# Two buffers for the token sums, and the low part of a pair's sums made inside the next pair's

## The chip, the cores and the metric

The kernel runs on one core of one Trainium2 chip. The metric is the device time of one launch in microseconds (us). Five engines work side by side: TensorE (PE in the views, its weight loads PEld), VectorE (DVE), ScalarE (ACT), GpSimd (POOL) and SyncE (SP), which issues most of the transfers.

## The reference

A decoder trunk over 256 tokens of width 2048: a recurrent block and an attention block, each followed by a dense layer with a squared ReLU (an MLP), all in float32. The change lies in the two MLPs alone:

```
def _mlp(h, w1, w2):
    u = jnp.einsum('bsd,df->bsf', h, w1)        # 2048 -> 8192
    u = jnp.square(jax.nn.relu(u))
    return jnp.einsum('bsf,fd->bsd', u, w2)     # 8192 -> 2048

for i in range(DEPTH):                          # DEPTH = 2
    ...                                         # recurrent block, then attention
    x = x + _mlp(_rmsnorm(x, mlp_norm[i]), mlp_w1[i], mlp_w2[i])
return _rmsnorm(x, final_norm)
```

## The kernel before

**High and low parts.** A float32 product is made of three products of rounded numbers: every operand is cut into a high part (ScalarE copies it into a rounded type, `whi` for a weight) and a low part (VectorE subtracts the high part from the original, `wlo`). `three` and `stand_w` then issue, for each 128 rows of the contraction, high by high, high by low and low by high. A weight comes in *units* of 128 x 2048 (1 MB) in tiles `raw`, or `q...` where sums of weights are made. `before_unit` and `behind_unit` run ahead of the unit in use: transfers five units ahead, `whi` three ahead, `wlo` two ahead. There are three buffers of `whi`, so the `whi` of the unit three places on is written when TensorE has finished the present one.

**The MLP.** It is done in eight parts, p = 0 to 7, of 1024 of the 8192 inner columns. In a *first* (the code's `"w"`, `plan_first`) one unit of w1 gives 128 inner columns for the 256 tokens: 48 matmuls of 256 columns into a bank `g` or `acc`. `u_done` then scales it and takes the ReLU on VectorE (`uu`, L517), squares it on ScalarE and copies the high part (`aT`); `u_low` makes the low part of it on VectorE one item later (L526).

**Sums of tokens and weights.** In parts 0 to 6 the second product is done by a scheme that needs seven products of half blocks where eight would be plain: `plan_group` names them b11, b21, t1, t2, b22, t3, t4, two groups per part, 12 matmuls of 512 columns each. t1, t2, b22 and t3 need sums of quarters of the tokens (s0 to s3), and some need sums of weights (`qT`, `q12`, `q21`, `q22`; L599 on VectorE, L595 by transfers that add). `sums_of_tokens` makes s0 to s3 for one of four pairs k of inner columns: four VectorE instructions of 128 x 128 into `sw`, then `hilo`: ScalarE's copy into the high half of `sT` (L203), and VectorE's subtraction into its low half (L204). `hilo` issues both in one go, so VectorE stands in front of its subtraction until ScalarE has copied. There are 2 MLPs x 7 parts x 4 pairs = 56 such pairs.

**The order** of a part is written out by hand in `ORDER[2]`: first, b11, t1, first, b21, b22, t2, first, t3, first, t4 (that is group 0), then group 1: b11, t1, first, b22, t2, b21, t3, first, first, first, t4. The firsts in it belong to the next part. In the main loop each item issues what runs ahead (`before_unit`), its matmuls (`fn`), `behind_unit`, what earlier items deferred (`after(n, ...)`), and then the sums of every pair that waits. The sums of part p+1 are held back until t3 of group 1 of part p has been issued (`busy`); the sums of pairs 0 and 1 then come together behind t3, those of pair 2 behind the second of the three firsts, and those of pair 3 behind t4, which is three items ahead of the t1 of the next part, where they are first read.

```
    0: ("s", "w") * 8,
    2: (
        "w", "b11 0", "t1 0", "w", "b21 0", "b22 0", "t2 0", "w", "t3 0", "w", "t4 0", "b11 1", "t1 1", "w",
        "b22 1", "t2 1", "b21 1", "t3 1", "w", "w", "w", "t4 1",
    ),
```

Each engine takes its instructions in the order in which they were issued.

Of the kernel before, what the change touches and what calls it, by code (L numbers as in the profile page):

```python
# [10 lines left out]
F32 = mybir.dt.float32  # L11
F32R = mybir.dt.float32r
AF = mybir.ActivationFunctionType
# [55 lines left out]
def trunk(ctx: ExitStack, tc: tile.TileContext, a: dict, out: bass.AP):  # L69
    nc = tc.nc  # L70
    P = 128
# [74 lines left out]
    def before_unit(i):  # L146
        step("load", i + 1 + LOOK_LOAD, load)
        step("make", i + LOOK_HI, make)
        step("hi", i + LOOK_HI, cut_hi)
        step("lo", i + 1 + LOOK_LO, cut_lo)  # L150

    def behind_unit(i):
        step("make", i + 1 + LOOK_HI, make)
        step("hi", i + 1 + LOOK_HI, cut_hi)
# [26 lines left out]
    lru = Scope()  # L181
# [18 lines left out]
    state = {}  # L200

    def hilo(hi_out, lo_out, src):
        nc.scalar.activation(hi_out, src, AF.Copy)  # L203
        nc.vector.tensor_sub(lo_out, src, hi_out.bitcast(F32))  # L204

    def new_xT(n):
        t = perm.tile([P, 4, 512], F32R, name=f"xT{n}")
        state["xT", n] = t
        return t
# [318 lines left out]
    def sums_of_tokens():  # L528

        if not waiting or (busy[0] is not None and busy[0] < waiting[0][0]):  # L530
            return
        p, k = waiting.pop(0)
        uu = squares.pop((p, k))
        (a11, a21), (a12, a22) = ((uu[:, h, 0:128], uu[:, h, 128:256]) for h in range(2))
        w = lru.tile([P, 4, 128], F32, name="sw")
        nc.vector.tensor_sub(w[:, 0], a22, a21)  # L536
        nc.vector.scalar_tensor_tensor(w[:, 1], w[:, 0], -1.0, a11, op0=OP.mult, op1=OP.subtract)  # L537
        nc.vector.scalar_tensor_tensor(w[:, 2], w[:, 1], -1.0, a12, op0=OP.mult, op1=OP.subtract)  # L538
        nc.vector.tensor_sub(w[:, 3], a11, a21)  # L539
        t = lru.tile([P, 8, 128], F32R, name=f"sT{k}")  # L540
        hilo(t[:, 0:4], t[:, 4:8], w)
        state["sT", p, k] = t
        return True

    def standing(p, what):

        def get(k):
            if what[0] == "a":
                t, h = int(what[1]) - 1, int(what[2]) - 1
                x = aT(8 * (p % 2) + 4 * h + k)  # L550
                return x[:, t * 128:(t + 1) * 128], x[:, 256 + t * 128:256 + (t + 1) * 128]
            x = state["sT", p, k]
            return x[:, int(what[1])], x[:, 4 + int(what[1])]
        return get
# [305 lines left out]
    for n in range(NCH):  # L860
        xg[n] = new_xg(n)
        rs = [wts.tile([P, UW], F32, name="raw", bufs=RAW_BUFS) for _ in range(3)] if n == 0 else rs
        for h in range(2 if n == 0 else 1):
            w = 2 if n == 0 else 4
# [10 lines left out]
        t = new_xT(n)  # L875
        for h in range(2 if n == 0 else 1):
            w = 2 if n == 0 else 4
# [76 lines left out]
    for at, (u, fn, kind) in enumerate(items):  # L954
        if u is None:
            fn()
            continue
        before_unit(u)
        state["border"] = kind is None and at + 1 < len(items) and items[at + 1][2] == "w"
        fn()  # L960
        behind_unit(least[at] - 1)
        for f, args in later.pop(now[0], []):
            f(*args)
        while sums_of_tokens():
            pass
        now[0] += 1
# [73 lines left out]
```

## Time and profile before

| | us |
|---|---|
| median of 3 runs (lowest, highest) | 2125.91 (2124.99, 2126.18) |
| the profiled execution | 2125.21 |
| its span, first to last instruction | 2123.4 |
| TensorE busy, of the span | 2096.7 (99%) |
| VectorE busy | 1708.7 (80%) |
| ScalarE busy | 1253.2 (59%) |

The first MLP lies at about 392 to 1059 us of the span, the second runs from about 1453 us to the end. In them a part from 1 on takes 83.04 to 83.3 us. Shares of busy time are means over the span; what holds TensorE up in one place is read from the order of time there.

### The profile page before, as it was taken

What the parts mean: (1) busy time and instruction counts of PE and PEld (TensorE: products, weight loads), DVE (VectorE), ACT (ScalarE), POOL (GpSimd) and SP (SyncE); (2) the same over time, 40 slices, a digit from 0 to 9 for tenths busy, and PEclk for the clock granted to TensorE, in tenths of its full rate; (3) what the DMA queues carried; (4) which work ended last, traced back from release to release, by engine and by line L of the source; (5) the groups of instructions that cost most, each with busy time, mean ns of one, the idle gap of its engine ahead of it and who ended that gap; (6) DMA issues with size and microseconds to landing.
All of it is one profiled execution on the core that took longest, in us unless ns stands there. A gap on an engine that the chain in (4) does not pass through costs nothing.

```text
span 2123.4 us, 32378 instructions
## 1 busy us (share of the span) xinstructions
PE 2096.7 (99%) x13529; PEld 1885.6 (89%) x13529; DVE 1708.7 (80%) x1836; ACT 1253.2 (59%) x1303; POOL 122.2 (6%) x92
## 2 busy tenths in 40 slices
PE   7999999999999999999999999999999999999997
PEld 7999988998989899899888888889989898998996
DVE  8898955699999999998555555556999999999985
ACT  5877755556665656656545544555565656566563
POOL 2121100000000000000000000000000000000002
PEclk9999999999999999999999999999999999999999
DMA  6665555677788778777554454446777887787773
GB/s 227 220 211 192 194 210 183 229 245 239 248 265 264 231 257 265 232 243 239 198 182 163 171 178 163 167 168 245 242 242 246 267 263 230 257 267 231 240 244 139
DMA packets 69778, 472.30 MB, mean 222 GB/s; under 512 B 7680, under 2 KB 8064, under 8 KB 14336
## 3 DMA queue, kind: packets, MB, share of 16 engines
q1 hardware_dynamic: 61568, 411.51, 52.5%
q0 software_dynamic: 8064, 58.72, 14.0%
q8 instruction: 106, 1.74, 0.3%
q14 instruction: 40, 0.33, 0.0%
HBM read 409.39 MB, written 2.10 MB: 194 GB/s over the span
## 4 chain that ended last, share of the span: by engine, by line
PE 64%; DVE 25%; issue 7%; ACT 3%; DMA 0%; SPq 0%; DVEq 0%; ACTq 0%
PE acc L187 42%; PE g L187 13%; DVE wlo L128 13%; PE tr L187 6%; DVE qT L599 3%; DVE xc L603 3%; ACT sT L203 2%; ACT whi L124 1%; DVE uu L517 1%; DVE aT L526 1%; DVE sw L537 1%; DVE sw L538 1%; DVE sw L536 1%; DVE sw L539 0%; DVE sT L204 0%
## 5 line engine op out<-in xcount | busy, mean ns | idle before, releaser
L124 ACT ACTIVATE whi<-raw 128x2048 fp32r<-128x2048 f32 (+2 forms) x306 | 567.1, 1855 | 425.0 <-PE acc L187 304.3
L128 DVE TENSOR_TENSOR wlo<-raw,whi 128x2048 fp32r<-128x2048 f32 (+2 forms) x306 | 683.5, 2238 | 137.1 <-ACT whi L124 136.9
L187 PE MATMUL g<-xT,whi 128*128 128x256 f32 (+1 forms) x3617 | 622.8, 277 | 0.0
L187 PEld LDWEIGHTS g<-xT,whi 128*128 128x128 f32 x3617 | 545.8, 188 | 0.0
L187 PE MATMUL g<-xT,wlo 128*128 128x256 f32 x1808 | 501.4, 277 | 0.8 <-DVE wlo L128 0.8
L187 PEld LDWEIGHTS g<-xT,wlo 128*128 128x128 f32 x1808 | 339.8, 188 | 2.6 <-DVE wlo L128 1.2
L187 PE MATMUL acc<-whi,aT 128*128 128x512 f32 x1056 | 335.0, 391 | 0.0
L187 PE MATMUL acc<-xT,whi 128*128 128x256 f32 x1764 | 303.7, 277 | 3.1 <-DVE xT L881 2.1
L128 DVE TENSOR_TENSOR wlo<-q,whi 128x2048 fp32r<-128x2048 f32 x112 | 256.1, 2287 | 22.5 <-ACT whi L124 22.5
L124 ACT ACTIVATE whi<-q 128x2048 fp32r<-128x2048 f32 x112 | 212.8, 1910 | 103.9 <-PE g L187 91.6
L187 PEld LDWEIGHTS acc<-xT,whi 128*128 128x128 f32 x1764 | 266.9, 188 | 4.8 <-DVE xT L881 2.5
L187 PE MATMUL acc<-xT,wlo 128*128 128x256 f32 x880 | 244.4, 278 | 8.0 <-DVE wlo L128 7.9
L187 PE MATMUL acc<-whi,xT 128*128 128x512 f32 x768 | 245.9, 396 | 0.0
L187 PEld LDWEIGHTS acc<-whi,aT 128*128 128x128 f32 x1056 | 198.3, 188 | 40.8
L187 PE MATMUL acc<-wlo,aT 128*128 128x512 f32 x528 | 205.8, 390 | 0.0
L124 ACT ACTIVATE whi<-qT 128x2048 fp32r<-128x2048 f32 x56 | 107.4, 1918 | 131.3 <-DVE qT L599 71.1
L187 PEld LDWEIGHTS acc<-xT,wlo 128*128 128x128 f32 x880 | 165.9, 189 | 9.3 <-DVE wlo L128 9.3
L187 PEld LDWEIGHTS acc<-whi,xT 128*128 128x128 f32 x768 | 144.3, 188 | 30.7
L187 PE MATMUL acc<-wlo,xT 128*128 128x512 f32 x384 | 150.4, 392 | 0.0
L187 PE MATMUL tr<-whi,sT 128*128 128x512 f32 (+1 forms) x490 | 148.7, 373 | 0.2
L187 PE MATMUL acc<-whi,sT 128*128 128x512 f32 (+1 forms) x476 | 147.9, 378 | 0.0
L187 PE MATMUL tr<-whi,aT 128*128 128x512 f32 (+1 forms) x460 | 145.1, 384 | 0.0
(176 smaller groups left out, 2439.2 us busy)
## 6 DMA issues: line engine op xcount, KB each, us to landing
raw<-in_w SPq DMA_DIRECT2D x172, 1024.0 KB, 5.9
q<-in_w SPq DMA_DIRECT2D x84, 1024.0 KB, 7.0
raw<-in_w_qkv SPq DMA_DIRECT2D x48, 1024.0 KB, 4.8
raw<-in_w_in SPq DMA_DIRECT2D x35, 1024.0 KB, 4.8
q<-q POOLq DMA_DIRECT2D x28, 1024.0 KB, 12.2
q<-qT POOLq DMA_DIRECT2D x28, 1024.0 KB, 7.0
raw<-in_w_out SPq DMA_DIRECT2D x20, 1024.0 KB, 4.7
raw<-in_w_o SPq DMA_DIRECT2D x16, 1024.0 KB, 4.8
```

Source lines behind the costliest of these rows:

```text
L124: nc.scalar.activation(split[i][0][:, s], r, AF.Copy)
L128: nc.vector.tensor_sub(split[i][1][:, s], r, split[i][0][:, s].bitcast(F32))
L187: nc.tensor.matmul(o, l, r, start=start, stop=stop, skip_group_check=True)
L203: nc.scalar.activation(hi_out, src, AF.Copy)
L517: nc.vector.scalar_tensor_tensor(uu, ps[:, :S], 0.0, state["rstdB"], op0=OP.max, op1=OP.mult)
L526: nc.vector.tensor_sub(t[:, 256:512], uu, t[:, 0:256].bitcast(F32))
L536: nc.vector.tensor_sub(w[:, 0], a22, a21)
L537: nc.vector.scalar_tensor_tensor(w[:, 1], w[:, 0], -1.0, a11, op0=OP.mult, op1=OP.subtract)
L538: nc.vector.scalar_tensor_tensor(w[:, 2], w[:, 1], -1.0, a12, op0=OP.mult, op1=OP.subtract)
L599: nc.vector.tensor_add(q[to], q[a], q[b])
L603: (nc.vector.tensor_add if sign > 0 else nc.vector.tensor_sub)(x, x, bank[b])
```

## The change

The tile of the sums gets two buffers. The fourth sum is issued second. ScalarE's copy is issued where it was, but VectorE's subtraction is kept for later: it is issued inside the sums of the next pair, between its third and its last instruction, or, where no sums come before, at the end of the next item.

```
-        w = lru.tile([P, 4, 128], F32, name="sw")
+        w = lru.tile([P, 4, 128], F32, name="sw", bufs=2)
         nc.vector.tensor_sub(w[:, 0], a22, a21)
+        nc.vector.tensor_sub(w[:, 3], a11, a21)
         nc.vector.scalar_tensor_tensor(w[:, 1], w[:, 0], -1.0, a11, op0=OP.mult, op1=OP.subtract)
+        low_of_sums()
         nc.vector.scalar_tensor_tensor(w[:, 2], w[:, 1], -1.0, a12, op0=OP.mult, op1=OP.subtract)
-        nc.vector.tensor_sub(w[:, 3], a11, a21)
         t = lru.tile([P, 8, 128], F32R, name=f"sT{k}")
-        hilo(t[:, 0:4], t[:, 4:8], w)
+        nc.scalar.activation(t[:, 0:4], w, AF.Copy)
         state["sT", p, k] = t
+        state["low"] = (t, w)
         return True
+
+    def low_of_sums():
+        if "low" in state:
+            t, w = state.pop("low")
+            nc.vector.tensor_sub(t[:, 4:8], w, t[:, 0:4].bitcast(F32))
@@ the main loop, behind an item's deferred work
+        low_of_sums()
         while sums_of_tokens():
             pass
```

The order of instructions changes on VectorE alone (elsewhere only line numbers do). At two places it reads as follows; the lines L536 to L550 of the changed kernel are those of the diff, in it L538 and L540 are the two sums that read another sum, L550 is the subtraction that was L204, and L606 and L610 are the former L599 and L603.

VectorE behind t3 of group 1, where pairs 0 (`sT_5095`) and 1 (`sT_5103`) are summed, before:

```order
L536 TENSOR_TENSOR sw<-uu 128x128
L537 SCALAR_TENSOR_TENSOR sw<-sw,uu 128x128
L538 SCALAR_TENSOR_TENSOR sw<-sw,uu 128x128
L539 TENSOR_TENSOR sw<-uu 128x128
L204 TENSOR_TENSOR sT_5095<-sw,sT_5095 128x512
L536 TENSOR_TENSOR sw<-uu 128x128
L537 SCALAR_TENSOR_TENSOR sw<-sw,uu 128x128
L538 SCALAR_TENSOR_TENSOR sw<-sw,uu 128x128
L539 TENSOR_TENSOR sw<-uu 128x128
L204 TENSOR_TENSOR sT_5103<-sw,sT_5103 128x512
L128 TENSOR_TENSOR wlo<-raw,whi 128x2048
L517 SCALAR_TENSOR_TENSOR uu<-g,rstdB 128x256
```

The same place now:

```order
L536 TENSOR_TENSOR sw<-uu 128x128
L537 TENSOR_TENSOR sw<-uu 128x128
L538 SCALAR_TENSOR_TENSOR sw<-sw,uu 128x128
L540 SCALAR_TENSOR_TENSOR sw<-sw,uu 128x128
L536 TENSOR_TENSOR sw<-uu 128x128
L537 TENSOR_TENSOR sw<-uu 128x128
L538 SCALAR_TENSOR_TENSOR sw<-sw,uu 128x128
L550 TENSOR_TENSOR sT_5095<-sw,sT_5095 128x512
L540 SCALAR_TENSOR_TENSOR sw<-sw,uu 128x128
L128 TENSOR_TENSOR wlo<-raw,whi 128x2048
L517 SCALAR_TENSOR_TENSOR uu<-g,rstdB 128x256
L550 TENSOR_TENSOR sT_5103<-sw,sT_5103 128x512
```

Pair 0's subtraction has gone into pair 1's sums, and pair 1's behind the low part of a unit and the ReLU of a first.

VectorE behind t4, where pair 3 (`sT_5322`) is summed, before; `wlo<-qT` is the low part of the unit of the coming t1, `uu` the ReLU of the first ahead of b11 and t1, and `wlo<-raw` the low part of the unit of the first behind t1:

```order
L536 TENSOR_TENSOR sw<-uu 128x128
L537 SCALAR_TENSOR_TENSOR sw<-sw,uu 128x128
L538 SCALAR_TENSOR_TENSOR sw<-sw,uu 128x128
L539 TENSOR_TENSOR sw<-uu 128x128
L204 TENSOR_TENSOR sT_5322<-sw,sT_5322 128x512
L128 TENSOR_TENSOR wlo<-qT,whi 128x2048
L517 SCALAR_TENSOR_TENSOR uu<-g,rstdB 128x256
L128 TENSOR_TENSOR wlo<-raw,whi 128x2048
```

The same place now:

```order
L536 TENSOR_TENSOR sw<-uu 128x128
L537 TENSOR_TENSOR sw<-uu 128x128
L538 SCALAR_TENSOR_TENSOR sw<-sw,uu 128x128
L540 SCALAR_TENSOR_TENSOR sw<-sw,uu 128x128
L128 TENSOR_TENSOR wlo<-qT,whi 128x2048
L517 SCALAR_TENSOR_TENSOR uu<-g,rstdB 128x256
L550 TENSOR_TENSOR sT_5322<-sw,sT_5322 128x512
L128 TENSOR_TENSOR wlo<-raw,whi 128x2048
```

Pair 3's subtraction now stands behind the low part for t1 and behind the ReLU of a first, and still ahead of the low part of the next unit.

## Rows read from the trace of the kernel before

**Rows 1.** The page, busy us, share of the span, instructions.

```profile
PE 2096.7 (99%) x13529; PEld 1885.6 (89%) x13529; DVE 1708.7 (80%) x1836; ACT 1253.2 (59%) x1303; POOL 122.2 (6%) x92
```

**Rows 2.** Windows, one part: its length, then busy us and instructions of each engine.

```profile
533.00:616.10 83.10, 82.88 (x561) 75.28 (x559) 78.13 (x77) 50.26 (x42) 3.42 (x4) 1.00 0.79 253
```

**Rows 3.** Timeline, TensorE, part 1 of the first MLP: start, us, instruction, idle before.

```profile
590.62 0.40 PE L187 MATMUL g<-xT,whi 128*128 128x256 f32 x2
...
596.08 0.39 PE L187 MATMUL tr<-whi,aT 128*128 128x512 f32 x1
...
598.82 0.39 PE L187 MATMUL acc<-whi,sT 128*128 128x512 f32 x1
599.35 0.50 PE L187 MATMUL acc<-wlo,sT 128*128 128x512 f32 x1
599.69 0.62 PE L187 MATMUL acc<-whi,sT 128*128 128x512 f32 x2
600.15 0.40 PE L187 MATMUL acc<-wlo,sT 128*128 128x512 f32 x1
...
610.18 0.39 PE L187 MATMUL acc<-whi,sT 128*128 128x512 f32 x1
610.62 0.50 PE L187 MATMUL acc<-wlo,sT 128*128 128x512 f32 x1
610.96 0.63 PE L187 MATMUL acc<-whi,sT 128*128 128x512 f32 x2
...
615.98 0.40 PE L187 MATMUL g<-xT,whi 128*128 128x256 f32 x2
616.29 0.38 PE L187 MATMUL g<-xT,wlo 128*128 128x256 f32 x1
616.51 0.40 PE L187 MATMUL g<-xT,whi 128*128 128x256 f32 x2
```

**Rows 4.** Timeline, TensorE, the first behind the first t1 of an MLP.

```profile
435.48 0.40 PE L187 MATMUL g<-xT,whi 128*128 128x256 f32 x2
436.27 0.39 PE L187 MATMUL g<-xT,wlo 128*128 128x256 f32 x1 [0.39 <-DVE wlo L128]
436.49 0.40 PE L187 MATMUL g<-xT,whi 128*128 128x256 f32 x2
```

**Rows 5.** Waits of TensorE's weight loads, 392 to 1004 us: total us, times, longest.

```profile
PEld acc L187 <- DVE wlo L128: 6.2, 12, 0.6
...
PEld g L187 <- DVE wlo L128: 0.6, 1, 0.6
```

**Rows 6.** Timeline, VectorE, the places of rows 3 and 4.

```profile
433.32 0.69 DVE L204 TENSOR_TENSOR sT<-sw,sT 128x512 fp32r<-128x512 f32 x1 [1.63 <-ACT sT L203]
...
595.42 0.28 DVE L539 TENSOR_TENSOR sw<-uu 128x128 f32<-128x128 f32 x1
596.40 0.69 DVE L204 TENSOR_TENSOR sT<-sw,sT 128x512 fp32r<-128x512 f32 x1 [0.70 <-ACT sT L203]
597.01 2.29 DVE L128 TENSOR_TENSOR wlo<-qT,whi 128x2048 fp32r<-128x2048 f32 x1
599.21 0.42 DVE L517 SCALAR_TENSOR_TENSOR uu<-g,rstdB 128x256 f32<-128x256 f32 x1
599.55 2.28 DVE L128 TENSOR_TENSOR wlo<-raw,whi 128x2048 fp32r<-128x2048 f32 x1
...
608.28 2.29 DVE L128 TENSOR_TENSOR wlo<-q,whi 128x2048 fp32r<-128x2048 f32 x1
...
613.95 2.29 DVE L128 TENSOR_TENSOR wlo<-raw,whi 128x2048 fp32r<-128x2048 f32 x1
```

**Rows 7.** The tile of the sums: ScalarE's copy (ns least/median/most), and who waited for it.

```profile
L203 ACT ACTIVATE sT<-sw x56: 615/632/636, 400.0 to 1990.5; 128x512 fp32r<-128x512 f32 x56
...
  DVE sT L204: 43.9, 56
```

**Rows 8.** Timeline, ScalarE, behind the copy of pair 3: the unit of the first behind t1.

```profile
596.27 1.91 ACT L124 ACTIVATE whi<-raw 128x2048 fp32r<-128x2048 f32 x1
```

## The prediction

> **What bounds the kernel now.** I read the page first: matmuls fill 99% of the span [rows 1], so the time is TensorE's, and only what makes its matmuls start earlier can change it. The windows by part come second. In one part of an MLP the matmuls are busy 82.88 of 83.10 us [rows 2]: 0.22 us of idle, which looks like no room. But a matmul's row is longer than its turn. At an even pace two matmuls of 512 columns start 0.46 us apart (599.69 to 600.15), 0.23 each, though a row lasts 0.39; and the 48 matmuls of a first take 596.08 - 590.62 = 5.46 us, 0.114 each, though one lasts 0.28 [rows 3]. A stall of a few tenths hides under the row in front of it. So the third view is the starts in the timeline, and there one part stalls at three places [rows 3]:
>
> - at t1 of group 0, 598.82 to 599.69 is 0.87 us for two matmuls that should take 0.46: 0.41 lost;
> - at b22 of group 0, 610.18 to 610.96 is 0.78 for 0.46: 0.32 lost;
> - at the first behind t2, 615.98 to 616.51 is 0.53 for three of 0.114: 0.19 lost.
>
> Each time the matmul that starts late reads `wlo`, and VectorE has just finished that tile: 597.01 + 2.29 = 599.30 against a start at 599.35; 608.28 + 2.29 = 610.57 against 610.62; 613.95 + 2.29 = 616.24 against 616.29 [rows 3, 6]. In each of the three the matmul after the late one is about 0.11 late as well; I count that in. In part 0 of an MLP there is one larger stall instead, in the first behind t1: 435.48 to 436.49 is 1.01 us for three matmuls, 0.67 lost [rows 4].
>
> The waits of the weight loads say how often: in the first MLP 12 on `wlo` for a bank `acc` and one for `g` [rows 5], that is two in each of parts 1 to 6 and the one of part 0; the second MLP has the same counts. (That view does not list the third, which is short.)
>
> Why is VectorE late? In front of each pair's subtraction it stands still for ScalarE's copy: 43.9 us in 56 pairs [rows 7], mostly 0.70, at the start of an MLP up to 1.63 [rows 6]. Around t1 it is the engine that is behind: the first ended on TensorE at 596.08 [rows 3], and VectorE comes to its ReLU at 599.21 [rows 6], 3.1 us later, with no idle row between 596.40 and there.
>
> **The change, part by part.**
>
> *The second buffer of `sw`* issues nothing. It lets pair 1's sums be written while pair 0's still wait to be subtracted. It costs room only.
>
> *The fourth sum moved to second place.* The same four instructions stand ahead of ScalarE's copy. The bounds are nothing and its whole 0.28 us [rows 6] per pair. I take nothing: what counts below does not need it.
>
> *The subtraction moved.* 56 x 0.69 us of work remain, none is added. Pair 0's now follows three of pair 1's sums, at some 0.28 each, which is 0.6 to 0.9 us behind the start of a copy that takes 0.63 [rows 6, 7]: a rest of 0 to 0.1 us in place of 0.70. Those of pairs 1 to 3 come a `wlo` (2.29) later, when the copy is long done: nothing left. So up to 2.8 us per part of standing still goes, over the four pairs.
>
> *At t1.* The least that must happen: of the four pairs only the last counts, VectorE being no earlier up to 595.70 (595.42 + 0.28). Then `wlo<-qT` starts there and not at 597.01, since both the 0.70 and the subtraction (596.40 to 597.01, 0.61 of queue) stood ahead of it [rows 6]. It ends at 597.99. TensorE wants it at 598.82 + 0.23 = 599.05 [rows 3]: 1.06 us to spare, the 0.41 goes. At the most it starts 2.8 + 0.61 = 3.4 us earlier.
>
> *Behind it* stand the ReLU and the subtraction of pair 3, then `wlo<-raw` for the first behind t1, at 599.55 now. By the least case the ReLU starts at 597.90 (0.09 before the end of `wlo<-qT`, as 599.21 to 599.30 now), the subtraction at 598.24, `wlo<-raw` at 598.85: 0.70 earlier [rows 6]. At the most it is bounded by ScalarE: the `whi` of this unit can start when TensorE has finished the first, 596.08, a little before its 596.27 now, and takes 1.91 [rows 3, 8], so it starts at about 598.05: 1.5 earlier. From there on I take VectorE's work as unchanged down to 613.95, so 0.7 to 1.5 us is what b22 and the next first may use. TensorE comes to b22 0.41 earlier and VectorE was 610.62 - 610.41 = 0.21 late there: 0.62 is needed, and either case gives it. At the first behind t2 TensorE comes 0.73 earlier, and VectorE was about 0.08 late (616.29 against 615.98 + 2 x 0.114): 0.81 is needed, which the least case misses by 0.1 and the most meets by 0.7. The pairs before the last have 2.1 us of waits to give, and their being of no use at all is unlikely; I take the most.
>
> *In part 0* VectorE waits 1.63 us in front of pair 3's subtraction [rows 6], and that subtraction too goes behind the ReLU, so `wlo<-raw` may come up to 1.63 + 0.61 = 2.2 us earlier. TensorE's stall there is 436.27 - 435.71 = 0.56 plus 0.11 [rows 4]: it goes.
>
> *The moved subtraction itself* is now late by how much? Pair 3 is read by the fourth quarter of t1, its low half by the last matmul of that: 598.82 + 11 x 0.23 = 601.3. By the least case it is done at 598.24 + 0.69 = 598.93. It is queued behind the ReLU, which waits for the first on TensorE (596.08): no matter, that is 1.8 us earlier than 597.90. It costs nothing while those 2.4 us last.
>
> **A rule and the rows.** The rows of busy time give an idle of 0.22 us a part, the starts give 0.41 + 0.32 + 0.19 = 0.92. The Trainium skill, Perfetto Trace Analysis (Identifying the Most-Contended Engine), says that busy time of matmuls is a poor measure of how near TensorE is to its limit, as they are pipelined. By that, this trace agrees: rows of 0.39 us start 0.23 apart. The busy rows would make the sum 14 x 0.22 = 3 us, the starts make it the one below.
>
> **The sum.** 12 parts (1 to 6 of both MLPs) x 0.92 = 11.0 us, taking the part of rows 3 for all, and 2 x 0.67 = 1.3 for part 0: 12.3 us off 2125.21, the profiled execution, whose span is 2123.4 (1.8 us lie outside it). The median of the runs is 0.7 higher, 2125.91; on that scale 2113.6.
>
> **The rivals.**
>
> *VectorE's freed time comes back as other waits (B).* Once it is no longer behind, it must wait for TensorE's results and ScalarE's `whi`, and b22 and the next first are left as they were; t1 and part 0 alone gain. For it: the earliest start of `wlo<-raw` is set by ScalarE. Against it: even the least case met b22. 12 x 0.41 + 1.3 = 6.2 us: 2119.7.
>
> *The change does not do what it says (C): nothing moves.* The waits of VectorE have cover after all, or the stalls pass to another late tile at the same places. For it: the idle of TensorE in the windows is 0.22 us a part, and 14 x 0.22 = 3.1 us is then all that there is, 2122.8 at best, which is within 0.2% (4.3 us, about what a measurement of this kernel can tell from no change). Against it: three ends of `wlo` that lie 0.05 us before three late starts. The Trainium skill, VectorE: DVE Perf Modes (Rules for kernel authors), advises to reduce the number of operations and not of semaphores; by that this change, which removes no operation, gives 0 and 2125.9. The trace does not agree where the semaphore is another engine's: 43.9 us of VectorE's idle stand in front of these 56 operations [rows 7].
>
> *Slower (D): the low half of pair 3 comes too late for t1.* It now stands behind a ReLU that needs TensorE's last first. VectorE is 3.1 us behind TensorE there at present; if, in the new order, it were over 2.4 us later than in my least case, t1 would stop in its fourth quarter in each of 12 parts. One us past that point is 12 us: 2137.9. Against it: nothing in the order lengthens VectorE's queue ahead of that place.
>
> **Chances.** The forecast 0.64, B 0.19, C 0.11, D 0.06. The predicted time is that of the forecast, 2113.6; its own range, by a third stall that stays in part (12 x 0.1) and by stalls up to 0.1 larger or smaller in the other parts, is 2111.5 to 2116. The range for 8 in 10 reaches up to B: 2111.5 to 2120. Faster by over 0.2% are the forecast and B, 0.83; within 0.2% C, 0.11; slower D, 0.06.
>
> **What will show it.** In the changed kernel's timeline: no idle of some 0.7 us ahead of L550; `wlo<-qT` ending over 1 us before t1's second matmul; the two matmuls at t1 and at b22 0.46 us apart and not 0.87 and 0.78; the waits of weight loads on `wlo` gone from both MLPs; a part of 82.1 to 82.4 us where it had 83.04 to 83.3. If t1 is clean and b22 is not, B holds. If VectorE's idle moves in front of `uu` or `wlo` and the starts of TensorE stay as they are, C. If t1's last matmul waits for L550, D. The prediction would be wrong above all if another engine, ScalarE's `whi` or a transfer, is close behind VectorE at these places, where no row of before shows by how much.

## The result, and the profile after

The changed kernel takes 2114.3 us (median of 4 runs, 2113.44 to 2115.05) beside 2125.97 of the kernel before: a ratio of 0.9945, 95% interval 0.9929 to 0.9961, 11.7 us less. 2113.6 was forecast. The chips of the experiments further down gave the kernel before 2123.4 to 2124.1, so runs are compared by their ratio to it on the same chip.

The page after, and the window of one part of the first MLP (from the three firsts in a row to the next three; columns as in [rows 2]):

```profile
PE 2090.8 (99%) x13529; PEld 1890.9 (89%) x13529; DVE 1703.0 (81%) x1836; ACT 1255.8 (59%) x1303; POOL 122.2 (6%) x92
```

```profile
490.78:572.89 82.11, 82.09 (x560) 75.38 (x559) 77.67 (x77) 50.47 (x42) 3.41 (x4) 1.00 0.80 256
```

A part that took 83.10 us [rows 2] takes 82.11, and TensorE's idle time in it is all but gone. VectorE still issues 77 instructions in a part; its busy time falls by 0.46 us (78.13 to 77.67), about what the shorter sums of four pairs save (4 x 0.12, worked out further down). VectorE's waits in one part, first before (488.44 to 571.54 us), then after (490.78 to 572.89): total us, times, longest:

```profile
DVE sT L204 <- ACT sT L203: 2.8, 4, 0.7
DVE wlo L128 <- ACT whi L124: 1.9, 3, 1.4
```

```profile
DVE wlo L128 <- ACT whi L124: 3.2, 5, 1.4
DVE uu L517 <- PE g L187: 1.1, 3, 0.4
```

So VectorE stands still almost as long as before, 4.3 us in place of 4.7, but at other places, where in parts 1 to 6 no matmul comes to wait for it. The timeline of TensorE at the three places of [rows 3], in the same part:

```profile
600.16 0.39 PE L187 MATMUL acc<-whi,sT 128*128 128x512 f32 x1
600.39 0.39 PE L187 MATMUL acc<-wlo,sT 128*128 128x512 f32 x1
600.62 0.62 PE L187 MATMUL acc<-whi,sT 128*128 128x512 f32 x2
...
611.08 0.39 PE L187 MATMUL acc<-whi,sT 128*128 128x512 f32 x1
611.31 0.39 PE L187 MATMUL acc<-wlo,sT 128*128 128x512 f32 x1
611.54 0.62 PE L187 MATMUL acc<-whi,sT 128*128 128x512 f32 x2
...
616.53 0.40 PE L187 MATMUL g<-xT,whi 128*128 128x256 f32 x2
616.77 0.28 PE L187 MATMUL g<-xT,wlo 128*128 128x256 f32 x1
616.89 0.39 PE L187 MATMUL g<-xT,whi 128*128 128x256 f32 x2
```

The starts at t1 and b22 are 0.46 us apart where they were 0.87 and 0.78, at the next first 0.36 where they were 0.53. VectorE there, which answers to [rows 6]:

```profile
575.44 0.29 DVE L536 TENSOR_TENSOR sw<-uu 128x128 f32<-128x128 f32 x1
575.64 0.29 DVE L537 TENSOR_TENSOR sw<-uu 128x128 f32<-128x128 f32 x1
575.84 0.30 DVE L538 SCALAR_TENSOR_TENSOR sw<-sw,uu 128x128 f32<-128x128 f32 x1
576.17 0.29 DVE L540 SCALAR_TENSOR_TENSOR sw<-sw,uu 128x128 f32<-128x128 f32 x1
...
594.98 2.28 DVE L128 TENSOR_TENSOR wlo<-qT,whi 128x2048 fp32r<-128x2048 f32 x1
597.63 0.42 DVE L517 SCALAR_TENSOR_TENSOR uu<-g,rstdB 128x256 f32<-128x256 f32 x1 [0.36 <-PE g L187]
597.97 0.68 DVE L550 TENSOR_TENSOR sT<-sw,sT 128x512 fp32r<-128x512 f32 x1
599.47 2.29 DVE L128 TENSOR_TENSOR wlo<-raw,whi 128x2048 fp32r<-128x2048 f32 x1 [0.81 <-ACT whi L124]
...
608.21 2.29 DVE L128 TENSOR_TENSOR wlo<-q,whi 128x2048 fp32r<-128x2048 f32 x1
...
613.87 2.29 DVE L128 TENSOR_TENSOR wlo<-raw,whi 128x2048 fp32r<-128x2048 f32 x1
```

The ReLU (L517) now waits 0.36 us for TensorE, where VectorE came to it 3.1 us late: it has caught up. No subtraction (L550) has more than 0.1 us of idle ahead of it. The low parts end ahead of their matmuls: 594.98 + 2.28 = 597.26 against 600.39, 610.50 against 611.31, 616.16 against 616.77.

The waits of the weight loads, 392 to 1004 us, which answer to [rows 5]:

```profile
PEld tr L187 <- issue: 2.9, 7, 0.4
PEld acc L187 <- DVE sT L550: 0.9, 1, 0.9
```

No wait on `wlo` is left, but there is a new one, once in each MLP: t1 of part 0 waits for the moved subtraction. TensorE and VectorE there:

```profile
437.18 0.39 PE L187 MATMUL acc<-wlo,sT 128*128 128x512 f32 x1
438.10 0.50 PE L187 MATMUL acc<-whi,sT 128*128 128x256 f32 x2 [0.53 <-DVE sT L550]
```

```profile
436.76 0.68 DVE L610 TENSOR_TENSOR xc<-xc,tr 128x512 f32<-128x512 f32 x1
437.36 0.69 DVE L550 TENSOR_TENSOR sT<-sw,sT 128x512 fp32r<-128x512 f32 x1
```

From 437.18 to 438.10 is 0.92 us for one matmul of 0.23, and the one behind is late by 0.11: 0.80 lost, where part 0 had lost 0.67 in the first behind t1 [rows 4].

### The profile page after: what moved, and what is told of

Read it like the earlier page. It is cut to its first block, busy times and chain, and to the rows that moved or that the text cites. A ratio compares the mean times of both kernels' runs of the same rounds, so it can differ in the third digit from the quotient of the medians.

```text
span 2113.0 us, 32396 instructions
## 1 busy us (share of the span) xinstructions
PE 2090.8 (99%) x13529; PEld 1890.9 (89%) x13529; DVE 1703.0 (81%) x1836; ACT 1255.8 (59%) x1303; POOL 122.2 (6%) x92
## 4 chain that ended last, share of the span: by engine, by line
PE 96%; DVE 2%; ACT 1%; issue 0%; DMA 0%; SPq 0%; DVEq 0%; ACTq 0%
PE acc L187 49%; PE g L187 30%; PE tr L187 14%; DVE wlo L128 1%; PE tr L228 0%; ACT whi L124 0%; DVE xT L888 0%; PE tr L704 0%; PE g L712 0%; DMA raw<-in_w_in 0%; PE tr L735 0%; PE g L745 0%; PE g L711 0%; PE g L744 0%; PE g L743 0%
## 5 line engine op out<-in xcount | busy, mean ns | idle before, releaser
L187 PE MATMUL acc<-xT,whi 128*128 128x256 f32 x1764 | 308.2, 280 | 2.3 <-ACT whi L124 1.5
```

The source lines that it names most:

```text
L187: nc.tensor.matmul(o, l, r, start=start, stop=stop, skip_group_check=True)
```

## The experiments

All are edits of the changed kernel. The length of a part is taken, as above, between the starts of the three firsts in a row; there are six such lengths in each MLP, and they hold parts 1 to 6. "Lost" compares with 82.12.

| run | median us | before beside it | ratio (95%) | a part, us |
|---|---|---|---|---|
| before | | | 1 | 83.10 to 83.30 |
| changed | 2114.3 | 2125.97 | 0.9945 (0.9929 to 0.9961) | 82.11 to 82.13 |
| changed, again | 2111.39 | 2123.43 | 0.9940 (0.9927 to 0.9954) | 82.10 to 82.14 |
| no delay | 2116.41 | 2124.11 | 0.9963 (0.9951 to 0.9976) | 82.47 to 82.51 |
| last pair | 2111.36 | 2124.11 | 0.9938 (0.9926 to 0.9951) | 82.11 to 82.13 |
| first pairs | 2110.87 | 2124.11 | 0.9943 (0.9930 to 0.9955) | 82.11 to 82.13 |
| old order | 2113.23 | 2123.43 | 0.9946 (0.9933 to 0.9958) | 82.09 to 82.13 |
| one buffer | 2114.21 | 2124.08 | 0.9951 (0.9938 to 0.9964) | 82.09 to 82.13 |
| one more | 2111.81 | 2124.08 | 0.9941 (0.9927 to 0.9955) | 82.09 to 82.13 |
| two more | 2150.12 | 2124.08 | 1.0120 (1.0105 to 1.0134) | 84.94 to 85.19 |
| item later | 2128.83 | 2124.08 | 1.0023 (1.0014 to 1.0033) | 83.47 to 83.77 |
| ahead | 2110.32 | 2124.11 | 0.9933 (0.9920 to 0.9947) | 82.13 |
| ahead, again | 2109.45 | 2123.43 | 0.9930 (0.9918 to 0.9942) | 82.10 to 82.14 |
| take later | 2106.77 | 2123.43 | 0.9918 (0.9904 to 0.9931) | 81.84 to 81.87 |

**No delay.** The two buffers and the new order alone.

```
-        nc.scalar.activation(t[:, 0:4], w, AF.Copy)
+        hilo(t[:, 0:4], t[:, 4:8], w)
-        state["low"] = (t, w)
```

> The two buffers and the new order of the four sums stay, but each pair's subtraction is issued right behind ScalarE's copy again. My theory: from the sums of tokens to the first behind t2 VectorE's queue is the late one, and what counts is how much earlier it gets. The four waits of 0.70 us come back; the new order alone makes the sums of a pair shorter (start of the first to the end of the last: 1.14 us before, 1.02 in the changed kernel), 0.48 a part. That covers t1 (0.31 late) and leaves b22 0.14 late instead of 0.21: some 0.4 us a part lost where it was 0.92, so about 2120, with idle of 0.7 us ahead of each subtraction and a clean t1. Rival: the order of the sums is worth nothing and the delay is all: 2125.9, t1 stalls 0.4 us.

VectorE, then TensorE at t1, then the waits of weight loads from 392 to 1004 us:

```profile
596.59 0.69 DVE L204 TENSOR_TENSOR sT<-sw,sT 128x512 fp32r<-128x512 f32 x1 [0.70 <-ACT sT L203]
597.20 2.28 DVE L128 TENSOR_TENSOR wlo<-qT,whi 128x2048 fp32r<-128x2048 f32 x1
```

```profile
599.64 0.39 PE L187 MATMUL acc<-whi,sT 128*128 128x512 f32 x1
599.87 0.39 PE L187 MATMUL acc<-wlo,sT 128*128 128x512 f32 x1
```

```profile
PEld acc L187 <- DVE wlo L128: 1.7, 6, 0.3
```

The 0.70 is back and t1 is clean all the same: 597.20 + 2.28 = 599.48 against 599.87. Of the 12 waits on `wlo` for a bank `acc` the six short ones at b22 are left; b22 loses 0.15 to 0.21 us there and the first behind t2 0.16 to 0.20. A part loses 0.35 to 0.39 us, as my theory had it (0.4). The order of four small instructions is worth 0.6 to 0.8 us a part, three fifths and more of the whole.

**Last pair, first pairs.** The subtraction is delayed for one kind of pair only; for the others it is issued at once.

```
         state["low"] = (t, w)
+        if k < 3:              # first pairs: k == 3
+            low_of_sums()
```

> The subtraction is kept for later for the last pair of four alone; pairs 0 to 2 are subtracted at once. My theory: with the new order of the sums (0.48 us a part) and the last pair's 0.70 and 0.61 out of the way, VectorE is 1.2 to 1.8 us earlier, and t1, b22 and the next first need at most 0.81: parts 1 to 6 are as clean as in the changed kernel, 2114.3, although three of four waits are back. Rival: each wait is worth its quarter of the gain: 2114.3 + 3/4 of 11.7 = 2123.

> The reverse: pairs 0 to 2 are subtracted later, the last pair at once. My theory: VectorE has caught up by the last pair's sums, so wlo for t1 ends 1.31 us later than in the changed kernel, about 1.8 us ahead of its matmul in place of 3.1, and the wlo behind it waits for ScalarE anyway: parts 1 to 6 stay clean. In part 0 the subtraction in the middle of t1 no longer waits (0.80 us lost there in the changed kernel, twice), but the first behind t1 stalls by about 0.55 again: 2113.5 to 2114.3. Rival: the wait of the last pair is the one that counts, as the least case of the prediction had it: t1 and b22 stall again, 2122 or more.

Both have parts of 82.11 to 82.13 us: three of the four waits may come back, or the last alone, and nothing shows. With the new order there is room for either. So the rivals of both, that each wait has its quarter of the gain or that the last one has it all, have fallen for a kernel that has the new order; with the old order the two were not tried. In part 0 the two differ as expected: the first stalls in t1 by 0.80 us, as the changed kernel does, the second in the first behind t1 by 0.67.

**Old order.** The delay with the four sums as they were.

```
-        nc.vector.tensor_sub(w[:, 3], a11, a21)
         ...
         nc.vector.scalar_tensor_tensor(w[:, 2], w[:, 1], -1.0, a12, op0=OP.mult, op1=OP.subtract)
+        nc.vector.tensor_sub(w[:, 3], a11, a21)
```

> The changed kernel with the four sums in their old order (the fourth last), the rest of the change kept. My theory: the delayed subtraction alone makes VectorE 1.3 us and more earlier at t1 and behind it, which is enough for all three places: parts 1 to 6 of 82.1 us as in the changed kernel, no measurable difference to it. Rival: the gain is that of the new order, which alone gave two thirds of it: about 2121 on a chip where the kernel before takes 2126.

0.9946, parts as clean: the delay is enough without the order. Each half of the change buys most of what the other does, and the two gains don't add up.

**One buffer.** The subtraction goes ahead of the next pair's sums, so the two pairs that come together wait once.

```
+        low_of_sums()
-        w = lru.tile([P, 4, 128], F32, name="sw", bufs=2)
+        w = lru.tile([P, 4, 128], F32, name="sw")
         ...
-        low_of_sums()
```

> One buffer of the sums again; a pair's subtraction is issued right ahead of the next pair's sums and not inside them. My theory: only the two pairs that come together lose something, 0.70 us of VectorE's queue in each part, which the slack behind it holds: 2114.3. Rival: the second buffer and the place in the middle are what the change is worth: 2118 or more.

The parts are those of the changed kernel: neither the second buffer nor the place in the middle of the sums is needed for the gain.

**One more, two more.** Idle work on VectorE behind each pair's sums, into a tile that nobody reads then.

```
+        spare = perm.tile([P, 512], mybir.dt.bfloat16, name="junk")
+        for _ in range(1):     # two more: 2
+            nc.vector.tensor_sub(spare.rearrange("p (q c) -> p q c", q=4), w, w)
```

> The changed kernel, with one more VectorE operation of 128 x 512 (0.69 us, 0.61 of queue) behind each pair's sums, whose result nobody reads. My theory: 2.4 us of queue a part come back, as much as the waits were, but VectorE has 1.9 us of idle in that stretch now (0.26, 0.49, 0.36 and 0.81): it is about 0.5 us later where b22 has 0.8 and the next first 0.6 us of slack. Parts 1 to 6 stay clean or nearly so; part 0 loses 0.6 more, twice: 2114.5 to 2117. Rival: VectorE's busy time sets the pace, and 56 x 0.61 us come on top: 2148. Another: queue taken by work undoes the change as the waits did: 2125.

> The same with two such operations behind each pair's sums, 4.9 us of queue a part. My theory: now the slack is gone: wlo for t1 comes about 1.0 us late, that for b22 1.0 more, the next first 0.2, with 0.1 us behind each: some 2.5 us in each of 12 parts and 2.4 us in part 0 together: about 2147. Rival: VectorE's idle elsewhere in the part takes it up, 2117 or less.

56 operations of 0.69 us cost the parts nothing; 112 cost 2.8 to 3.1 us a part. VectorE and TensorE at t1 with two more:

```profile
602.91 2.28 DVE L128 TENSOR_TENSOR wlo<-qT,whi 128x2048 fp32r<-128x2048 f32 x1
```

```profile
603.40 0.39 PE L187 MATMUL acc<-whi,sT 128*128 128x512 f32 x1
605.25 0.50 PE L187 MATMUL acc<-wlo,sT 128*128 128x512 f32 x1 [1.46 <-DVE wlo L128]
```

The low part ends at 605.19 and the matmul that wants it starts at 605.25, 1.6 us late (1.0 was expected). So it is VectorE's queue that sets the stalls, waits and work alike, and the change has bought a slack of at least one such operation per pair and less than two.

**Item later.** In parts 1 to 6 the left-over subtraction waits one item more.

```
+        state["due"] = now[0] + (2 if p else 1)
-        low_of_sums()
+        if now[0] >= state.get("due", 0):
+            low_of_sums()
```

> In parts 1 to 6 the subtraction that is left over is issued one item later still (behind the b11 ahead of t1, for the last pair). My theory: in the changed kernel it ends 4.0 us ahead of the last matmul of t1 that reads it; one item later it stands behind another wlo, an addition to xc and a subtraction, would end about 0.68 us late, and t1 loses some 0.8 us in its fourth quarter in each of 12 parts: 2123 to 2124. Rival: VectorE gets there earlier as well, nothing is lost: 2114.3.

The fourth quarter of t1, then VectorE:

```profile
599.72 0.39 PE L187 MATMUL acc<-wlo,sT 128*128 128x512 f32 x1
601.23 0.50 PE L187 MATMUL acc<-whi,sT 128*128 128x256 f32 x2 [1.12 <-DVE sT L551]
```

```profile
600.49 0.68 DVE L551 TENSOR_TENSOR sT<-sw,sT 128x512 fp32r<-128x512 f32 x1
```

The last matmul of t1 waits for the subtraction, 1.28 us and 0.11 behind it, more than the 0.8 that I expected: I had counted one addition to `xc` ahead of it, and there are two (0.60 us each). The mechanism of rival D is real; the changed kernel stands one item away from it.

**Ahead.** The left-over subtraction goes to the start of the next item's work.

```
         before_unit(u)
+        low_of_sums()
         ...
-        low_of_sums()
         while sums_of_tokens():
```

> The subtraction that is left over is issued at the start of the next item's own work, behind the low part of a unit and ahead of the ReLU, not at the item's end. My theory: in part 0 the last matmuls of the first t1 wait 0.69 us (with the one behind, 0.80) for the subtraction because it stands behind a ReLU and an addition to the tile xc that need TensorE's results; ahead of them it is ready in time, both stalls go, and parts 1 to 6 stay as they are: 1.6 us less, 2112.7. Rival: the first t1 waits for VectorE in whatever order, the stall moves to the first behind it: 2114.3.

> The kernel with the subtraction at the start of the next item once more, beside the changed kernel on the same chip. My theory: 1.6 us less than the changed kernel, all of it in part 0 of the two MLPs. Rival: no difference.

The changed kernel beside it:

> The changed kernel itself once more, so that the runs beside it stand against it on the same chip. By all theories 0.9945 of the kernel before, within its interval.

VectorE and TensorE in part 0:

```profile
435.73 0.68 DVE L550 TENSOR_TENSOR sT<-sw,sT 128x512 fp32r<-128x512 f32 x1
...
436.67 0.68 DVE L610 TENSOR_TENSOR xc<-xc,tr 128x512 f32<-128x512 f32 x1
```

```profile
436.49 0.39 PE L187 MATMUL acc<-wlo,sT 128*128 128x512 f32 x1
436.71 0.40 PE L187 MATMUL acc<-whi,sT 128*128 128x256 f32 x2
```

The subtraction ends at 436.41, ahead of the matmul at 436.71, and both stalls of part 0, in t1 and in the first behind it, are gone from the trace. From the first ahead of b11 to the three firsts in a row, part 0 takes 63.03 us (426.05 to 489.08) where the changed kernel takes 64.04 (426.74 to 490.78): 1.0 us in each MLP, more than the 0.80 expected, as the first behind the stalled t1 had been slow to its end too (5.65 us in place of 5.46). On one chip it took 2109.45 against 2111.39 of the changed kernel; the intervals of the two ratios overlap, so that the clock agrees with the trace and doesn't prove it.

**Take later.** That kernel, and b22's bank is added to `xc` two items later.

```
-TAKES = {"b11": 0, "b21": 0, "t1": 0, "t2": 0, "b22": 0, "t3": 0, "t4": 2}
+TAKES = {"b11": 0, "b21": 0, "t1": 0, "t2": 0, "b22": 2, "t3": 0, "t4": 2}
```

> The kernel with the subtraction at the start of the next item, and besides the addition of b22's bank to the tile xc made two items later. It aims at the only stall that is left in a part: t3 of group 1 starts 0.17 us late and the matmul behind it 0.08, because it writes on in the bank that t2 left, and VectorE's addition of that bank to xc is queued behind the one of b22 (0.60 us of queue) and a wlo. My theory: with b22's out of the way the bank is read 0.60 us earlier, the 0.25 go in each of 14 parts: 3.5 us less than the same kernel without it. Rival: t3 waits for something else of that stretch (its weights, the weight load), nothing changes.

TensorE at t3 of group 1 in the changed kernel, where t3 starts 0.40 us behind the matmul before it and not 0.23:

```profile
487.55 0.39 PE L187 MATMUL acc<-whi,aT 128*128 128x512 f32 x1
487.95 0.47 PE L187 MATMUL tr<-whi,sT 128*128 128x512 f32 x1
```

The same place with b22's bank added later, then the addition of the bank that t2 left:

```profile
568.39 0.39 PE L187 MATMUL acc<-whi,aT 128*128 128x512 f32 x1
568.62 0.39 PE L187 MATMUL tr<-whi,sT 128*128 128x512 f32 x1
```

```profile
567.67 0.68 DVE L610 TENSOR_TENSOR xc<-xc,tr 128x512 f32<-128x512 f32 x1
```

The addition ends at 568.35, and t3 follows on at the even 0.23. A part falls to 81.84 to 81.87 us, 0.26 in each of the 12 parts measured (3.6 us if all 14 gain it): the rival falls by the trace. On the clock it took 2106.77 against 2109.45 of the same kernel without it, 2.7 us less; the two intervals overlap, so the clock agrees here too and doesn't prove it. By its median this is the fastest of the kernels, 0.9918 of the kernel before.

## Why the prediction was right

**The bound and the stalls.** TensorE's starts and not its busy time held the gain, and all three stalls went in all 12 parts (t1 takes 2.73 us there, b22 2.72 and the first behind t2 5.46, where the part of [rows 3] took 3.16, 3.07 and 5.83). Rival C is out: the idle of the windows had offered 0.22 us a part, the part lost 1.0 us.

**The path through VectorE.** At the most, `wlo<-raw` was to start 1.97 us behind the end of the first on TensorE, held by ScalarE; it starts 2.04 behind it (597.43 in the timeline, to 599.47), with 0.81 us of idle that ScalarE's `whi` ends. From there 0.9 us of slack (1.5 - 0.62) were left at b22 and 0.7 (1.5 - 0.81) at the next first by the prediction; 0.81 and 0.61 were measured. Rival B, that the freed time comes back as waits and b22 stays late, had its waits right (0.36 and 0.81 here, 4.3 us of waits in a part where it had 4.7) and their effect wrong.

**The sum, point by point.** The profiled executions show it by stage. Parts 1 to 6 of the two MLPs take 12.9 us less together (498.80 to 492.74 and 499.57 to 492.69) where 11.0 was predicted. Part 0, from the first ahead of b11 to the three firsts, takes 0.17 us more in the first MLP (63.87 to 64.04) and 0.19 more in the second, where 0.67 less was predicted. So the MLPs gained 12.6 us where 12.3 was forecast: the mechanism of parts 1 to 6 was right, but that the sum is so near is luck, as one error of 1.9 us too little and one of 1.7 too much nearly cancel. This execution of the changed kernel also lost some 2.2 us ahead of the first MLP's part 0 (426.74 against 424.57 at that first), in its first 40 us (the last section).

**The steps that failed.**

- "*that subtraction too goes behind the ReLU*" for part 0. The order of parts 1 to 6 was read into part 0. There the sums of the last pair come only two items ahead of t1, so the subtraction goes to the end of b11, behind an addition to `xc` that reads b11's bank. Rival D's mechanism holds there. The run with the subtraction ahead shows it: moved in front of that addition it costs nothing.
- "*The same four instructions stand ahead of ScalarE's copy ... I take nothing*". The new order alone gives 0.6 to 0.8 us a part and makes t1 clean. It did not change the sum, since the delay alone suffices. The starts in the changed kernel show what it is: an instruction starts 0.20 us behind the one before it although that lasts 0.29, but 0.33 behind when it reads its result (575.44, 575.64, 575.84, 576.17). Before, two of the four read the result just ahead of them; now one does, and the sums of a pair take 1.02 us in place of 1.14. The second and third sum before, where the third reads the second and starts 0.33 behind it:

```profile
574.40 0.29 DVE L537 SCALAR_TENSOR_TENSOR sw<-sw,uu 128x128 f32<-128x128 f32 x1
574.73 0.29 DVE L538 SCALAR_TENSOR_TENSOR sw<-sw,uu 128x128 f32<-128x128 f32 x1
```

- The stall at the first behind t2 was mis-sized: 0.19 us by its first three matmuls, 0.37 by the whole unit, in the very part of [rows 3] (5.83 us from 615.98 to the next unit at 621.81, where 5.46 is the rule). The matmuls behind the stall keep a slower pace to the end of the unit, of which the last section tells. Six of the 12 units do so; in the other six the unit loses 0.15 to 0.20. Over the 12 parts this stall cost 3.3 us where the sum has 2.3; the other two varied from part to part (t1 0.41 to 0.48 us, b22 0.31 to 0.39) and cost 9.5 where the sum, which took one part for all, has 8.8.

The Trainium skill, VectorE: DVE Perf Modes (Rules for kernel authors), has it that each of several chained operations empties the pipe in any case, and that one should cut their number and not the semaphores. The runs here do not agree for this place: with the number unchanged, a new order of four gave 0.37% and taking away the wait on another engine 0.54% (the kernels with the new order and with the delay alone).

## What to carry to other kernels

When one engine is the bound at 99%, measure its room by the starts of its instructions against an even pace; the busy share hides stalls of tenths of a microsecond, and the ones removed here were 1.0 to 1.2 us in each part. An engine that stands still for another in the middle of a critical queue is freed by putting its next work between; how far to delay is given by the reader, and must be read off for every variant of the loop, its first turn too. Before adding two remedies for one wait, test each alone: here the order alone gave two thirds of the gain and the delay alone all of it, and with the new order the delay of the last pair, or of the other three, was enough.

## What the runs showed of the hardware

A stalled matmul costs more than its wait. In each of the three stalls on `wlo` of [rows 3] the following matmul of the same width was 0.11 us late too; and in some firsts the pace stayed lower for the rest of the unit. In the kernel before, the unit of the stall at 616.29 ends where the next one starts:

```profile
621.81 0.39 PE L187 MATMUL tr<-whi,sT 128*128 128x512 f32 x1
```

From 616.51 [rows 3] to there, 45 matmuls take 5.30 us, 0.118 each. One part earlier the same first has the same stall (0.54 us for its first three matmuls, where the other took 0.53):

```profile
532.87 0.40 PE L187 MATMUL g<-xT,whi 128*128 128x256 f32 x2
...
533.41 0.28 PE L187 MATMUL g<-xT,whi 128*128 128x256 f32 x1
...
538.52 0.39 PE L187 MATMUL tr<-whi,sT 128*128 128x512 f32 x1
```

There the 45 matmuls behind it take 5.11 us, 0.114 each, which is the even pace. The slow unit takes 5.83 us, this one 5.65. Of the 12 units six are of the slow kind, and they lie in the six parts of 83.25 to 83.30 us; the other six lie in those of 83.10 to 83.14. Why the pace stays lower in one and not in the other was not tried.

The start of an execution moves its time, and the granted clock alone does not say by how much. The first 40 us of the profiled execution of the changed kernel, then of the same kernel run again (columns as in [rows 2]; the seventh is the granted clock):

```profile
0.00:40.00 40.00, 31.64 (x181) 27.39 (x182) 32.65 (x55) 23.24 (x43) 13.45 (x11) 0.83 0.68 235
```

```profile
0.00:40.00 40.00, 33.42 (x214) 29.80 (x215) 34.22 (x64) 23.87 (x46) 16.12 (x11) 0.96 0.72 246
```

181 matmuls were done at 0.83 of the clock and 214 at 0.96. But the kernel before did 199 in that time, "take later" 186 and "ahead, again" 215, all three at 0.96 as well, so something else counts too, which was not tried. In these two runs of the changed kernel the three firsts of part 0 began at 490.78 and 487.53 us, while the parts behind agree to 0.04 us. So a change of 2 us in these parts is sure in the trace and not in the medians.
